# Grouped-query attention worked in pairs of heads, with its output GEMM given out between the pieces

## The chip, the core and the metric

The kernel runs on one core of one Trainium2 chip. The metric is the device time of one execution in microseconds (us); lower is better. The core's engines each work through a list of their own in program order and wait for each other at semaphores: PE (TensorE: matmuls and transposes), ACT (ScalarE), DVE (VectorE), POOL (GpSimd) and SP (SyncE, which here issues the weights' DMAs). PE has two clock levels, 1.2 and 2.4 GHz; the profile gives the granted clock as a share of the higher one, so 0.50 is the lower level and 1.00 the higher.

## The reference

The reference is two blocks one after the other on 256 tokens of width 1024: a hybrid block (differential attention, gated convolution, memory attention, an MLP), then two layers modulated by adaLN vectors. The change touches one step of the second block's first layer, grouped-query attention with 16 query heads of 64 features and 4 key/value heads, each of which serves 4 query heads:

```
def gqa_attention(h, w_qkv, q_g, k_g, w_o, cos, sin):
    B, T, _ = h.shape
    qkv = h @ w_qkv
    q, k, v = jnp.split(qkv, [Q_WIDTH, Q_WIDTH + KV_WIDTH], axis=-1)
    q = apply_rope(rmsnorm(q.reshape(B, T, N_HEADS, HEAD_DIM), q_g), cos, sin)
    k = apply_rope(rmsnorm(k.reshape(B, T, N_KV_HEADS, HEAD_DIM), k_g), cos, sin)
...
        s = jnp.einsum('bqkgd,bskd->bkgqs', q_blk, k).astype(jnp.float32) * scale
        p = jax.nn.softmax(s, axis=-1).astype(v.dtype)
        return jnp.einsum('bkgqs,bskd->bqkgd', p, v)
...
    return o @ w_o
```

## The kernel before

**Weights and GEMMs.** Every weight is streamed from HBM in loads of 1 MB and split into `whi` (rounded to fp32r, a cast on ACT, L86) and `wlo` (the exact rest, a subtraction on DVE, L87). The class `Weights` keeps these splits a few ahead of their use (`W.pump`, `W.rest`), and `W.cap` holds the order of the splits back where a stage has no use for them. A large GEMM makes three matmuls for each pair of operands (`mm3`, L397 to L399: hi by hi, hi by lo, lo by hi), each on 128x128 weights and 512 columns. The class `Rows` is a GEMM that goes by rows of the weights: `run(k, ...)` adds the k-th of eight blocks of 128 rows to four accumulators of [128, 512] in the pool `ps_a`. For the first two blocks it makes both token tiles at once; from the third block on it makes the first token tile up to block 5, holds the rest back, and makes it at the end, so that the first token tile is finished early and its normalisation can start (`L295` are the transposes of that).

**Attention, before.** After the projection of q, k and v, the 16 heads go one by one through five pieces. `gq_a` makes the scores of a head (L1254; operands of 64 rows, half of the array, both token tiles into one bank of `ps_a`), the negated row maximum `nm` (L752, DVE), the `bias` (L755, DVE) and two exponentials with row sums (L757, ACT, into `p`). `gq_b` makes the reciprocal of the sums (`rec`, L762, DVE) and scales the two halves of `p` by it (L764, DVE). `gq_t` transposes `p` by four matmuls with the identity (L771, PE) and copies the result into `pT` (L773, ACT). `gq_o` multiplies by the values (L1274, PE; an output of 64 columns, half of the array) and `gq_os` splits the finished pair of heads into the GEMM's operands `omT` hi (L277, a cast on ACT) and lo (L278, a subtraction on DVE). These matmuls are of plain fp32, and each is two passes in the profile: `x4` of L1254 or L1274 is two matmuls.

The function `slots` sets the order. In slot j, the AV product of head j-5, the transposes of head j-3, the scores of head j, the scaling of head j-1 and the split of head j-5 are issued in this order, which is also the order on every engine:

```
    slots(16, [[(5, gq_o), (3, gq_t), (0, gq_a), (1, gq_b), (5, gq_os)]])
```

The first few slots run as fillers inside the projection's last chunk, the others in a loop behind it, and only when all are through does the output GEMM `Rows("o2", 8)` start, with 96 matmuls on `omT`. The second half of q's rotary embedding (`rope`, L1191 to L1193, on DVE, and its transposes L680 on PE) falls between the first slots. The stage behind the output GEMM is the MLP `m2`, whose first matmul is of line L447.

Of the kernel before, what the change touches and what calls it, by code (L numbers as in the profile page):

```python
# [17 lines left out]
NT = 2  # L18
# [5 lines left out]
class Weights:  # L24
    """The weights in the order of their use: 1 MB loads, each split in two halves into
    operands hi (rounded to float32r) and lo (the exact rest)."""
# [66 lines left out]
    def first(self, kind, key):  # L93
        """The index of the first half of a load."""
        return 2 * next(i for i, u in enumerate(self.plan) if u[:2] == (kind, key))
# [8 lines left out]
    def done(self, rest=True):  # L104
        """One more half is used up: go on with the loads and splits (lo only up to rest() if told so)."""
# [7 lines left out]
def kernel(  # L113
# [28 lines left out]
    # ------------------------------------------------------------------ the weights' order  # L142
# [53 lines left out]
    # ------------------------------------------------------------------ loads at the start  # L196
# [63 lines left out]
    # ------------------------------------------------------------------ helpers  # L260
    def rsqrt(ss, inv, y, E=None):
        """y = 1/sqrt(ss*inv + EPS) by Newton's steps from the usual first guess."""
# [26 lines left out]
    def transposed(t, xn, gcol, bcol, dst):  # L289
        """A function that makes dst[hi, lo][:, :, tokens t] = (xn * g + b)^T, xn in two halves."""  # L290
# [38 lines left out]
    def norm(t, src, ssp, gcol, bcol, dst, E=None):  # L329
        """dst[hi, lo][:, :, tokens t] = (src over its root mean square * g + b)^T with g, b per feature;  # L330
        ssp: the sums of squares of src's halves. In three parts: this one, and two to be called later."""
# [32 lines left out]
    def later(n, f):  # L364
        """f runs n ticks on."""
        due.append((clock[0] + n, f))
# [40 lines left out]
    def gemm_cols(key, n0, act, evac, fill=1, acc=None, i0=0):  # L407
        """512 columns: act^T (tokens on partitions out) @ w; evac(the token tiles' psums)."""
# [13 lines left out]
    def gap():  # L422
        """A product that may run while TensorE would wait for operands."""
# [3 lines left out]
    def gemm_cols_skew(key, n0s, act, evacs, second, fill=1):  # L427
        """The first two of some chunks of columns: the first token tile runs six halves of weights
        ahead, while second() makes the operands of the other."""
# [36 lines left out]
    def gemm_cols_start(key, n0, act, evac, second, fill=1):  # L466
        """The first columns: two halves of weights for a token tile in turn; second() makes the operands
        of the other."""
# [22 lines left out]
    def gemm_feat(key, f0, act, p=ps_a, fill=1):  # L491
        """256 features: w^T @ act (features on partitions out), in one bank [2, 256 tokens]."""
# [765 lines left out]
    def gq_b(h):  # L1258
        softmax_b(*gq[h])
# [212 lines left out]
```

## Time and profile before

| | |
|---|---|
| Time, median of 3 runs | 1336.67 us |
| The three runs | 1336.67, 1340.35 and 1336.23 us |
| Span of the profiled execution | 1335.7 us (the profile gives no other time of it) |
| PE busy | 1315.5 us, 98% of the span |
| DVE, ACT busy | 926.9 us (69%), 731.2 us (55%) |
| Mean granted clock of PE | 0.992 |

The share of busy time is an average over many stages. The grouped-query attention and its output GEMM take some 73 us of the span, and what the change is worth has to be read from these 73 us. Start times in a timeline are us from the span's start. A matmul's "took" time overlaps its neighbours; what it costs in a chain is the distance from its start to the next start. In a timeline row the bracket at the end says how long the engine stood idle ahead of the row and what released it.

### The profile page before, as it was taken

What the parts mean: (1) busy time and instruction counts of PE and PEld (TensorE: products, weight loads), DVE (VectorE), ACT (ScalarE), POOL (GpSimd) and SP (SyncE); (2) the same over time, 40 slices, a digit from 0 to 9 for tenths busy, and PEclk for the clock granted to TensorE, in tenths of its full rate; (3) what the DMA queues carried; (4) which work ended last, traced back from release to release, by engine and by line L of the source; (5) the groups of instructions that cost most, each with busy time, mean ns of one, the idle gap of its engine ahead of it and who ended that gap; (6) DMA issues with size and microseconds to landing.
All of it is one profiled execution on the core that took longest, in us unless ns stands there. A gap on an engine that the chain in (4) does not pass through costs nothing.

```text
span 1335.7 us, 20533 instructions
## 1 busy us (share of the span) xinstructions
PE 1315.5 (98%) x7883; PEld 1141.9 (85%) x7883; DVE 926.9 (69%) x1424; ACT 731.2 (55%) x1184; POOL 140.0 (10%) x375
## 2 busy tenths in 40 slices
PE   8899999999999999999899999999999999999998
PEld 6788789999998889987657889987789988799896
DVE  5555678755776778777776787676888877764453
ACT  6765665554444655445575755445646543674451
POOL 1522154500001000100400000000000000000000
PEclk8999999999999999999899999999999999999999
DMA  6572344456885788984313687894886765465650
GB/s 235 201 247 95 127 149 163 154 199 217 269 273 173 237 293 288 285 305 144 110 63 111 200 297 254 269 315 151 292 269 222 253 229 194 135 208 187 214 190 32
DMA packets 166959, 275.43 MB, mean 206 GB/s; under 512 B 8412, under 2 KB 95244, under 8 KB 166732
## 3 DMA queue, kind: packets, MB, share of 16 engines
q1 hardware_dynamic: 137260, 219.78, 48.7%
q10 hardware_dynamic: 27808, 50.41, 11.5%
q0 software_dynamic: 1792, 3.92, 1.1%
q8 instruction: 62, 1.02, 0.3%
q14 instruction: 37, 0.30, 0.1%
HBM read 273.04 MB, written 1.05 MB: 205 GB/s over the span
## 4 chain that ended last, share of the span: by engine, by line
PE 93%; DMA 2%; POOL 1%; DVE 1%; ACT 1%; issue 1%; SPq 0%; ACTq 0%; DVEq 0%; POOLq 0%
PE bank L397 15%; PE bank L399 15%; PE bank L398 15%; PE bank L497 12%; PE bank L499 12%; PE bank L498 12%; PE bank L447 2%; PE bank L1274 1%; PE bank L1254 1%; PE bank L1386 1%; PE bank L438 1%; PE bank L771 1%; PE bank L295 1%; PE bank L680 1%; PE bank L1034 1%
## 5 line engine op out<-in xcount | busy, mean ns | idle before, releaser
L86 ACT CAST whi<-raw 128x1024 fp32r<-128x1024 f32 x412 | 426.3, 1051 | 277.1 <-PE bank L399 79.7
L87 DVE TENSOR_TENSOR wlo<-raw,whi 128x1024 fp32r<-128x1024 f32 x412 | 496.3, 1220 | 90.7 <-ACT whi L86 89.6
L497 PE MATMUL bank<-hT,whi 128*128 128x256 f32 x1152 | 328.6, 285 | 0.0
L499 PE MATMUL bank<-hT,wlo 128*128 128x256 f32 x1152 | 324.8, 282 | 0.0
L498 PE MATMUL bank<-hT,whi 128*128 128x256 f32 x1152 | 324.5, 282 | 0.0
L497 PEld LDWEIGHTS bank<-hT,whi 128*128 128x128 f32 x1152 | 216.5, 188 | 1.9 <-issue 1.3
L498 PEld LDWEIGHTS bank<-hT,whi 128*128 128x128 f32 x1152 | 217.5, 189 | 0.6
L499 PEld LDWEIGHTS bank<-hT,wlo 128*128 128x128 f32 x1152 | 217.1, 188 | 0.0
L397 PE MATMUL bank<-whi,act 128*128 128x512 f32 x384 | 152.2, 396 | 0.0
L398 PE MATMUL bank<-wlo,act 128*128 128x512 f32 x384 | 151.7, 395 | 0.0
L399 PE MATMUL bank<-whi,act 128*128 128x512 f32 x384 | 151.6, 395 | 0.0
L397 PE MATMUL bank<-whi,hT 128*128 128x512 f32 x308 | 128.2, 416 | 0.8 <-ACT hT L321 0.8
L399 PE MATMUL bank<-whi,hT 128*128 128x512 f32 x308 | 122.7, 398 | 0.0
L398 PE MATMUL bank<-wlo,hT 128*128 128x512 f32 x308 | 122.5, 398 | 0.0
L1018 DVE SCALAR_TENSOR_TENSOR acc<-araw,cond,acc 128x512 f32<-128x512 f32 x128 | 95.6, 747 | 27.4 <-DMA araw<-in_ada_w_dram 27.0
L399 PEld LDWEIGHTS bank<-whi,act 128*128 128x128 f32 x384 | 72.0, 187 | 17.5
L397 PEld LDWEIGHTS bank<-whi,act 128*128 128x128 f32 x384 | 72.0, 187 | 17.0
L398 PEld LDWEIGHTS bank<-wlo,act 128*128 128x128 f32 x384 | 72.0, 188 | 16.9
L397 PEld LDWEIGHTS bank<-whi,hT 128*128 128x128 f32 x308 | 58.3, 189 | 18.8 <-ACT hT L321 4.2
L399 PEld LDWEIGHTS bank<-whi,hT 128*128 128x128 f32 x308 | 58.4, 190 | 15.1 <-DVE hT L310 1.0
L398 PEld LDWEIGHTS bank<-wlo,hT 128*128 128x128 f32 x308 | 58.5, 190 | 13.5 <-issue 0.7
L278 DVE TENSOR_TENSOR act<-s,act 128x512 fp32r<-128x512 f32 x36 | 24.9, 691 | 58.2 <-ACT act L277 58.2
(298 smaller groups left out, 1893.9 us busy)
## 6 DMA issues: line engine op xcount, KB each, us to landing
araw<-in_ada_w_dram ACTq DMA_DIRECT2D x192, 256.0 KB
raw<-in_w_in_dram SPq DMA_DIRECT2D x40, 1024.0 KB
raw<-in_mlp_w_in_dram SPq DMA_DIRECT2D x32, 1024.0 KB
raw<-in_mlp_w_out_dram SPq DMA_DIRECT2D x32, 1024.0 KB
raw<-in_gmlp_w_in_dram SPq DMA_DIRECT2D x24, 1024.0 KB
raw<-in_w_mlp_in_dram SPq DMA_DIRECT2D x16, 1024.0 KB
raw<-in_w_mlp_out_dram SPq DMA_DIRECT2D x16, 1024.0 KB
raw<-in_gmlp_w_out_dram SPq DMA_DIRECT2D x12, 1024.0 KB
```

The source lines that it names most:

```text
L86: self.nc.scalar.copy(hv, v)
L87: self.rests.append(lambda v=v, hv=hv, lv=lv: self.nc.vector.tensor_sub(lv, v, hv.bitcast(F32)))
L278: V.tensor_sub(lo, src, hi.bitcast(F32))
L295: T.transpose(pss[g][:, j * P:(j + 1) * P], xn[g][:, j * P:(j + 1) * P], ident)
L397: T.matmul(acc, xh, wh, start=start, stop=False)
L398: T.matmul(acc, xh, wl, start=False, stop=False)
L399: T.matmul(acc, xl, wh, start=False, stop=stop)
L447: T.matmul(acc[c][0], act[e][:, k, 0:P], w[0][:, j, :], start=(k + e == 0), stop=False)
L497: T.matmul(acc[:, j], wh[:, k, :], act[0][:, k, :], start=(k == 0), stop=False)
L498: T.matmul(acc[:, j], wh[:, k, :], act[1][:, k, :], start=False, stop=False)
L499: T.matmul(acc[:, j], wl[:, k, :], act[0][:, k, :], start=False, stop=(k == 7))
L1018: V.scalar_tensor_tensor(acc, ada_st.pop(j), cond[:, k:k + 1], acc, op0=ALU.mult, op1=ALU.add)
```

## The change

Two heads are worked as one pair, eight pairs in all. `gq_scores` makes the scores of two heads in turn, one in the upper and one in the lower 64 rows of the array, each head into a bank of its own in the pool `ps_x`, then both `nm` and one `bias` for the pair. `gq_exp` makes the pair's four exponentials, `gq_norm` one reciprocal and four scalings, `gq_turn` the eight transposes, with one copy to `pT` on ACT and the other on DVE (before: both on ACT). `gq_out` multiplies both heads by the values, one in the left and one in the right 64 columns of the array, and splits the pair. `gq_pieces` sets three pieces for each j: the scores of pair j; the transposes of pair j-1 with the exponentials of pair j; the AV product of pair j-2 with the scaling of pair j. The output GEMM's block k starts as soon as pair k is through, and a piece is given out between its parts. Since the four accumulators of that GEMM now stand in `ps_a` at the same time, scores, transposes and AV products share the four banks of `ps_x`. The rest of the full diff takes out comments and docstrings. Its core:

```
@@ -503,10 +503,10 @@
         return acc
 
     class Rows:
-        def __init__(self, key, nk, skew=6):
-            self.key, self.nk, self.skew = key, nk, skew
+        def __init__(self, key, nk, skew=6, between=None):
+            self.key, self.nk, self.skew, self.between = key, nk, skew, between
             self.acc = None
             self.held = []
...
@@ -528,6 +528,8 @@
                 if k < self.nk - self.skew:
                     for t in range(NT):
                         self.mm(k, w, act, j, t)
+                        if self.between and t == 0:
+                            self.between()
                     W.done()
                     tick(fill)
                 else:
...
@@ -1247,65 +1249,96 @@
 
     gq = {}
 
-    def gq_a(h):
-        ps = bank(ps_a).rearrange("p (t k) -> p t k", t=2)
-        pr = slice(64 * (h % 2), 64 * (h % 2) + 64)
+    def gq_scores(p):
+        pss = [bank().rearrange("p (t k) -> p t k", t=2) for _ in range(2)]
         for t in range(NT):
-            T.matmul(ps[:, t], qT2[pr, h // 2, t * P:(t + 1) * P], kT2[pr, h // 4, :], start=True, stop=True)
-        p = attnp.tile([P, 2, 256], F32, tag="p", name="p", bufs=4)
-        gq[h] = p, softmax_a(ps, rsq2[:, :, h], p)
-    def gq_b(h):
-        softmax_b(*gq[h])
-    def gq_t(h):
-        pT = attnp.tile([P, 2, 256], F32, tag="pT", name="pT", bufs=3)
-        transpose_p(gq[h][0], pT.rearrange("p a b -> p (a b)"))
-        gq[h] = pT
-    def gq_o(h):
-        if h % 2 == 0:
-            gq["o"] = bank()
-        ps = gq["o"]
-        pT = gq.pop(h)
-        o0 = 64 * (h % 2)
-        kv = h // 4
+            for c in range(2):
+                pr = slice(64 * c, 64 * c + 64)
+                T.matmul(pss[c][:, t], qT2[pr, p, t * P:(t + 1) * P], kT2[pr, p // 2, :], start=True, stop=True)
+        nm = small.tile([P, 2, 2], F32, tag="nmg", name="nm")
+        for c in range(2):
+            V.tensor_reduce(nm[:, c], pss[c], axis=AX.X, op=ALU.max, negate=True)
+        bias = small.tile([P, 2, 2], F32, tag="biasg", name="bias")
+        V.tensor_mul(bias, nm, rsq2[:, :, 2 * p:2 * p + 2].rearrange("p t c -> p c t"))
+        gq[p] = pss, bias
+    def gq_exp(p):
+        pss, bias = gq[p]
+        sums = small.tile([P, 2, 2], F32, tag="sumsg", name="sums", bufs=4)
+        pt = [attnp.tile([P, 2, 256], F32, tag="p", name="p", bufs=4) for _ in range(2)]
+        for c in range(2):
+            for t in range(NT):
+                S.activation(pt[c][:, t], pss[c][:, t], AF.Exp, bias=bias[:, c, t:t + 1],
+                             scale=rsq2[:, t, 2 * p + c:2 * p + c + 1], accum_out=sums[:, c, t:t + 1])
+        gq[p] = pt, sums
+    def gq_norm(p):
+        pt, sums = gq[p]
+        rec = small.tile([P, 2, 2], F32, tag="recg", name="rec")
+        V.reciprocal(rec, sums)
+        for c in range(2):
+            for t in range(NT):
+                V.tensor_scalar(pt[c][:, t], pt[c][:, t], rec[:, c, t:t + 1], None, op0=ALU.mult)
+    def gq_turn(p):
+        pT = [attnp.tile([P, 2, 256], F32, tag="pT", name="pT", bufs=4) for _ in range(2)]
+        for c in range(2):
+            transpose_p(gq[p][0][c], pT[c].rearrange("p a b -> p (a b)"), on_act=(c == 0))
+        gq[p] = pT
+    def gq_out(p):
+        pT = gq.pop(p)
+        ps = bank()
+        vs = slice(64 * (p // 2), 64 * (p // 2) + 64)
         for kb in range(2):
-            T.matmul(ps[o0:o0 + 64, 0:256], v2[:, kb, 64 * kv:64 * kv + 64], pT[:, kb], start=(kb == 0), stop=(kb == 1))
-        gq[h, "o"] = ps
-    def gq_os(h):
-        ps = gq.pop((h, "o"))
-        if h % 2:
-            split_to(oT2[0][:, h // 2, :], oT2[1][:, h // 2, :], ps[:, 0:256])
+            for c in range(2):
+                T.matmul(ps[64 * c:64 * c + 64, 0:256], v2[:, kb, vs], pT[c][:, kb], start=(kb == 0), stop=(kb == 1))
+        split_to(oT2[0][:, p, :], oT2[1][:, p, :], ps[:, 0:256])
+    def gq_pieces():
+        for j in range(10):
+            for stage in ((gq_scores, 0, None, 0), (gq_turn, 1, gq_exp, 0), (gq_out, 2, gq_norm, 0)):
+                fs = [(f, j - lag) for f, lag in (stage[:2], stage[2:]) if f and 0 <= j - lag < 8]
+                if fs:
+                    yield j - 2 if stage[0] is gq_out else -1, fs
 
     rate, clock[1] = clock[1], 0.0
     fillers.append(rope_tables)
     W.cap = W.first("D", ("o2", 0))
     gemm_cols_skew("qkv2", (1024, 0), hT, (evac_kv2, evac_q2(0)), end)
-    fillers.extend([lambda: None] * 3)
-    slots(16, [[(5, gq_o), (3, gq_t), (0, gq_a), (1, gq_b), (5, gq_os)]])
     W.rest()
-    W.cap += 0
     gemm_cols("qkv2", 512, hT, evac_q2(1))
-    clock[1] = 0
-    n = 0
-    while fillers:
-        n += 1
-        if n > 2:
-            W.cap += 1
-            W.pump()
-            W.rest(1)
+    pieces = deque(gq_pieces())
+    def piece():
+        if pieces:
+            for f, p in pieces.popleft()[1]:
+                f(p)
+        W.cap += 1
+        W.pump()
+        W.rest(1)
         tick()
-    W.cap = 1 << 30
+    rows = Rows("o2", 8, between=piece)
+    for k in range(8):
+        while any(0 <= p <= k for p, _ in pieces):
+            piece()
+        piece()
+        if k == 2:
+            W.cap = 1 << 30
+            while len(ada) > 96:
+                ada.popleft()()
+        end = rows.run(k, [(oT2, k)], residual((0, 0), mods(0, 1)))
     clock[1] = 0.95
-    end = Rows("o2", 8).run(0, [(oT2, k) for k in range(8)], residual((0, 0), mods(0, 1)))
     g_st.close()
     end = mlp("m2i", "m2o", residual((0, 1), mods(1, 0)), end)
     ada_flush(48)
     clock[1] = 0.8
 
-    # ------------------------------------------------------------------ gated MLP with mixing over tokens
     gm_st = ExitStack()
     gmp = pool(gm_st, "gmlp")
     vg = gmp.tile([P, 2, 3072], F32, name="vg")
```

The lines of the two kernels differ: the scores are L1254 before and L1258 after, `nm` L752 and L1261, `bias` L755 and L1263, the exponentials L757 and L1272, `rec` L762 and L1279, the scalings of `p` L764 and L1282, the transposes L771 and L773, the copies of `pT` L773 and L775 (ACT) with L777 (DVE), and the AV product L1274 and L1297. In these rows a matmul counts once, not by its passes.

On DVE, one slot in the middle of the attention before, followed by the start of the next:

```order
L752 TENSOR_REDUCE nm<-bank 128x2
L755 TENSOR_TENSOR bias<-nm,rsq_6769 128x2
L762 RECIPROCAL rec<-sums 128x2
L764 TENSOR_SCALAR p<-p,rec 128x256 x2
L278 TENSOR_TENSOR omT_780<-bank,omT_779 128x256
L87 TENSOR_TENSOR wlo<-raw,whi 128x1024
L752 TENSOR_REDUCE nm<-bank 128x2
```

And on DVE in the middle of the attention now, one pair and the start of the next:

```order
L1279 RECIPROCAL rec<-sums 128x4
L1282 TENSOR_SCALAR p<-p,rec 128x256 x4
L1261 TENSOR_REDUCE nm<-bank 128x2 x2
L1263 TENSOR_TENSOR bias<-nm,rsq_6769 128x4
L777 COPY pT<-bank 128x512
L87 TENSOR_TENSOR wlo<-raw,whi 128x1024
L278 TENSOR_TENSOR omT_780<-bank,omT_779 128x256
L1279 RECIPROCAL rec<-sums 128x4
```

Before, `nm` and `bias` of a head stood ahead of the reciprocal and the scalings of the head before it. Now `nm` and `bias` of a pair stand behind the reciprocal and the scalings of the pair before it, and the subtraction that makes `omT` lo stands ahead of that reciprocal.

On ACT, two slots in the same place before:

```order
L757 ACTIVATE p,sums<-bank,bias,rsq_6769 128x256 x2
L86 CAST whi<-raw 128x1024
L773 COPY pT<-bank 128x512
L757 ACTIVATE p,sums<-bank,bias,rsq_6769 128x256 x2
L277 CAST omT_779<-bank 128x256
L773 COPY pT<-bank 128x512
```

And on ACT now, a pair with a weight's cast and a pair with the two DMA issues of the adaLN weights (L1001):

```order
L1272 ACTIVATE p,sums<-bank,bias,rsq_6769 128x256 x4
L86 CAST whi<-raw 128x1024
L277 CAST omT_779<-bank 128x256
L1001 DMA araw<-in_ada_w_dram 128x512 x2
L775 COPY pT<-bank 128x512
L1272 ACTIVATE p,sums<-bank,bias,rsq_6769 128x256 x4
```

The cast of `omT` hi stands behind the four exponentials of a later pair, and behind the weight's cast where there is one.

The start of the attention, on DVE before (L1191 to L1193 are the rotary embedding of q's second half):

```order
L752 TENSOR_REDUCE nm<-bank 128x2
L755 TENSOR_TENSOR bias<-nm,rsq_6769 128x2
L1191 TENSOR_TENSOR hf<-q_7109,ropeg 128x256 x2
L1192 TENSOR_TENSOR q_7109<-q_7109,ropeg 128x512
L1193 TENSOR_TENSOR q_7109<-q_7109,hf 128x512
L752 TENSOR_REDUCE nm<-bank 128x2
L755 TENSOR_TENSOR bias<-nm,rsq_6769 128x2
L762 RECIPROCAL rec<-sums 128x2
```

And the start on DVE now (the embedding is L1193 to L1195 here):

```order
L1195 TENSOR_TENSOR q_7109<-q_7109,hf 128x512
L87 TENSOR_TENSOR wlo<-raw,whi 128x1024
L1279 RECIPROCAL rec<-sums 128x4
L1282 TENSOR_SCALAR p<-p,rec 128x256 x4
L87 TENSOR_TENSOR wlo<-raw,whi 128x1024
L1193 TENSOR_TENSOR hf<-q_7109,ropeg 128x256 x2
L1194 TENSOR_TENSOR q_7109<-q_7109,ropeg 128x512
L1195 TENSOR_TENSOR q_7109<-q_7109,hf 128x512
L1261 TENSOR_REDUCE nm<-bank 128x2 x2
L1263 TENSOR_TENSOR bias<-nm,rsq_6769 128x4
```

Ahead of these rows stand the first pair's two `nm`, its `bias` and the first half of the embedding, as before. Between the first and the second pair's `nm` there are now two subtractions of `wlo` and the first pair's scalings; before, the second head's `nm` followed the embedding at once.

On PE, the start of the attention before (L680 are the transposes of the second half of q):

```order
L1254 MATMUL bank<-kT_6767,qT_6766 128x256 x6
L771 MATMUL bank<-ident,p 128x128 x4
L1254 MATMUL bank<-kT_6767,qT_6766 128x256 x2
L680 MATMUL bank<-ident,q_7109 128x128 x4
L771 MATMUL bank<-ident,p 128x128 x4
L1254 MATMUL bank<-kT_6767,qT_6766 128x256 x2
L1274 MATMUL bank<-pT,v_6768 64x256 x2
```

And on PE now, from the transposes of the first pair to the first part of the output GEMM (L682 is the L680 of before):

```order
L773 MATMUL bank<-ident,p 128x128 x8
L682 MATMUL bank<-ident,q_7109 128x128 x4
L1258 MATMUL bank<-kT_6767,qT_6766 128x256 x4
L773 MATMUL bank<-ident,p 128x128 x8
L1297 MATMUL bank<-pT,v_6768 64x256 x4
L1258 MATMUL bank<-kT_6767,qT_6766 128x256 x4
L397 MATMUL bank<-whi,omT_779 128x512
L398 MATMUL bank<-wlo,omT_779 128x512
L399 MATMUL bank<-whi,omT_780 128x512
L397 MATMUL bank<-whi,omT_779 128x512
L398 MATMUL bank<-wlo,omT_779 128x512
L399 MATMUL bank<-whi,omT_780 128x512
```

From here on a pair's transposes, AV product and scores and six of the GEMM's matmuls follow each other in turn. Six of the GEMM's matmuls stand in each pair's turn, 48 of the 96 in all; the other 48 come behind the last pair.

## Rows read from the trace of the kernel before

**Rows 1.** The page: the chain that ended last by engine, one costly group

```profile
PE 93%; DMA 2%; POOL 1%; DVE 1%; ACT 1%; issue 1%; SPq 0%; ACTq 0%; DVEq 0%; POOLq 0%
...
L1018 DVE SCALAR_TENSOR_TENSOR acc<-araw,cond,acc 128x512 f32<-128x512 f32 x128 | 95.6, 747 | 27.4 <-DMA araw<-in_ada_w_dram 27.0
```

**Rows 2.** Three stretches, us from the start: busy time of each engine, PE's clock

```profile
core 0: us, PE busy (x) PEld busy (x) DVE busy (x) ACT busy (x) POOL busy (x), PEclk, DMA share, GB/s
664.00:674.00 10.00, 10.00 (x29) 6.11 (x28) 8.00 (x19) 8.35 (x19) 1.91 (x4) 0.55 0.03 4
674.00:706.00 32.00, 32.00 (x150) 18.68 (x150) 23.00 (x67) 23.89 (x66) 0.00 (x0) 1.00 0.19 65
706.00:731.00 25.00, 25.00 (x114) 20.17 (x115) 15.91 (x30) 11.34 (x21) 0.00 (x0) 1.00 0.41 135
```

**Rows 3.** Timeline of PE: attention's start, a steady slot, the output GEMM, the next stage

```profile
663.03 1.08 PE L771 MATMUL bank<-ident,p 128*128 128x128 f32 x4 [3.51 <-DVE p L764]
664.05 2.07 PE L1254 MATMUL bank<-kT,qT 64*128 64x256 f32 x4
...
676.22 1.13 PE L1254 MATMUL bank<-kT,qT 64*128 64x256 f32 x4
677.27 1.08 PE L1274 MATMUL bank<-pT,v 128*64 128x256 f32 x4
678.28 0.65 PE L771 MATMUL bank<-ident,p 128*128 128x128 f32 x4
678.87 1.13 PE L1254 MATMUL bank<-kT,qT 64*128 64x256 f32 x4
...
707.72 0.50 PE L397 MATMUL bank<-whi,omT 128*128 128x512 f32 x1
708.07 0.40 PE L398 MATMUL bank<-wlo,omT 128*128 128x512 f32 x1
...
730.55 5.78 PE L447 MATMUL bank<-whi,hT 128*128 128x512 f32 x24
```

**Rows 4.** Timeline of PE: a pair of heads in row halves, differential attention

```profile
186.98 0.93 PE L866 MATMUL bank<-kT,qT 64*128 64x128 f32 x8
187.84 0.38 PE L497 MATMUL bank<-hT,whi 128*128 128x256 f32 x1
```

**Rows 5.** Timeline of DVE: attention's start, one slot, an `omT` lo

```profile
658.50 0.68 DVE L752 TENSOR_REDUCE nm<-bank 128x2 f32<-128x512 f32 x1
...
659.40 0.77 DVE L1191 TENSOR_TENSOR hf<-q,ropeg 128x256 f32<-128x256 f32 x2
...
661.54 0.68 DVE L752 TENSOR_REDUCE nm<-bank 128x2 f32<-128x512 f32 x1
...
681.33 0.68 DVE L752 TENSOR_REDUCE nm<-bank 128x2 f32<-128x512 f32 x1
682.05 0.16 DVE L755 TENSOR_TENSOR bias<-nm,rsq 128x2 f32<-128x2 f32 x1
...
682.32 0.61 DVE L764 TENSOR_SCALAR p<-p,rec 128x256 f32<-128x256 f32 x2
682.85 1.22 DVE L87 TENSOR_TENSOR wlo<-raw,whi 128x1024 fp32r<-128x1024 f32 x1
683.99 0.68 DVE L752 TENSOR_REDUCE nm<-bank 128x2 f32<-128x512 f32 x1
...
686.53 0.42 DVE L278 TENSOR_TENSOR omT<-bank,omT 128x256 fp32r<-128x256 f32 x1 [0.86 <-ACT omT L277]
```

**Rows 6.** Timeline of ACT: one slot's exponentials and cast, an `omT` hi

```profile
682.31 0.56 ACT L757 ACTIVATE p<-bank,bias,rsq 128x256 f32<-128x256 f32 x1 [1.05 <-DVE rec L762]
...
682.86 0.55 ACT L757 ACTIVATE p<-bank,bias,rsq 128x256 f32<-128x256 f32 x1
...
683.41 1.04 ACT L86 CAST whi<-raw 128x1024 fp32r<-128x1024 f32 x1
...
686.13 0.36 ACT L277 CAST omT<-bank 128x256 fp32r<-128x256 f32 x1
```

## The prediction, made before the changed kernel was run

> **What bounds the kernel now.** I read the page first: PE ends 93% of the chain that ended last [rows 1]. That is a share over the whole span, so I went to the 73 us of grouped-query attention by windows and by PE's timeline. The reader is to see three stretches there. Until 663.03 PE has scores to make but then stands idle for 3.51 us, because the transposes wait for the first scaled `p` of DVE [rows 3]. From 664 to 674 PE is busy all the time, but at a granted clock of 0.55, which is the 1.2 GHz level for most of it; four passes of the scores took 2.07 us there against 1.13 us later [rows 2, 3]. From 674 to 731 PE is busy all the time at clock 1.00, while DVE is busy 23.00 of 32 us and ACT 23.89 of 32 [rows 2]. So the steady part is bound by PE. A slot costs 2.65 us of PE (676.22 to 678.87): 1.05 us for the scores, 1.01 for the AV product, 0.59 for the transposes [rows 3]. The other two engines use three quarters of it, a head at a time, with a slack that a pipeline over five heads can use.
>
> The output GEMM takes 707.72 to 730.55, that is 22.83 us for 96 matmuls and one set of eight transposes [rows 3], or about 0.23 us a matmul (22 us for the 96, the rest for the transposes). The next stage begins at 730.55, again with matmuls, and since PE ends 93% of the whole chain [rows 1], I take it that a shift of this point is kept to the end. **What the change is worth is how far this 730.55 moves.**
>
> **What it removes from PE.** Two heads in the two halves of the array run side by side. The trace has this already in differential attention: eight passes of L866, four of 128 and four of 256 columns, start at 186.98 and the next matmul at 187.84, so they took 0.86 us [rows 4]. Four passes of 256 columns alone cost 1.05 us here and four of 128 columns (the transposes) 0.59 us [rows 3], 1.64 us one after the other. So a pair costs a little over half, and I take the scores of a pair at 1.05 us where two heads cost 2.10, and in the same way the AV products at 1.01 us instead of 2.02. Over eight pairs that is 8 x (1.05 + 1.01) = 16.5 us less work on PE. Column halves of this shape do not stand in these rows; the bounds are 1.01 us (as with row halves) and 2.02 us (no gain). I take the first and keep the second as a rival. The GEMM's matmuls and the transposes cost the same as before: a pair's share on PE is 1.05 + 1.01 + 2 x 0.59 + 6 x 0.23 = 4.6 us.
>
> **What it adds, on DVE and ACT.** No operation is added there; eight of 16 `bias` and eight of 16 reciprocals fall away. What moves is their order, and here I part from PE's sum. Before, `nm` and `bias` of a head are ahead of the scalings of the head before it, so ACT always had the next exponentials to do while DVE scaled. Now, on DVE, a pair's `nm` and `bias` stand behind the reciprocal and the scalings of the pair before, which wait for that pair's last exponential; and the subtraction for `omT` lo stands ahead of the reciprocal and waits for the cast of `omT` hi, which on ACT stands behind these same four exponentials. So ACT and DVE take turns and nothing of one pair lies beside the next. One turn, by starts:
>
> - reciprocal to first scaling: `bias`, reciprocal and hand-over together take 682.05 to 682.32; 0.2 us for one of the two;
> - four scalings: two take 682.32 to 682.85, so 2 x 0.53 = 1.06 us;
> - two `nm`: about 0.6 us for the first and 0.72 for the second up to `bias` (681.33 to 682.05), 1.32 us [rows 5];
> - `bias` to the first exponential: 682.05 to 682.31, 0.26 us [rows 5, 6];
> - four exponentials: 682.31, 682.86, 683.41, so 4 x 0.55 = 2.20 us;
> - `omT` hi, from its start to that of the subtraction: 686.13 to 686.53, 0.40 us [rows 5, 6];
> - the subtraction: 0.42 us long, 0.34 up to the next instruction [rows 5].
>
> The sum is 5.78 us, more than PE's 4.6. So PE will wait about a microsecond in each pair, and the loop of the two other engines sets the pace.
>
> Some pairs cost more. A weight's cast in ACT's row ahead of `omT` hi adds about 1.0 us (1.04 us long) [rows 6]; by the order that is so in two pairs, the fourth and the fifth. Behind the fifth, ACT issues two loads of adaLN weights; the second refills a buffer that DVE must first read, in an instruction of 0.75 us like L1018's [rows 1], and this stands behind `nm` and `bias`. The copy of `pT` and the exponentials stand behind these issues on ACT, so the sixth pair costs about 1.3 us more. On SP and POOL nothing changes places.
>
> **The sum.** Everything up to the first score matmul is as before, and so is the first `nm` at 658.50 [rows 5].
>
> - First reciprocal: 658.50 + 1.32 (two `nm`) + 0.1 (`bias`) + 2.14 (half an embedding, 659.40 to 661.54) + 1.14 (`wlo`, 682.85 to 683.99) = 663.2 [rows 5].
> - Second reciprocal: 0.2 + 1.06 + 1.14 (`wlo`) + 2.14 (embedding) + 1.32 + 0.26 + 2.20, and 0.4 to hand the sums over = 8.7, so 671.9.
> - Third: 0.2 + 1.06 + 1.14 (`wlo`) + 1.32 + 0.26 + 2.20 + 0.40 + 0.34 = 6.9, so 678.8. The first part of the output GEMM begins here, and not before.
> - Fourth and fifth, with a cast: 2 x 6.8, so 692.4. Sixth: 7.1, so 699.5. Seventh and eighth: 2 x 5.8, so the last reciprocal is at 711.1.
> - Then the last scalings (1.26) and the last four transposes (0.6) to 713.0; six matmuls of the GEMM (1.4) cover the copy of `pT`; 714.4; the last two pairs' AV products, 2 x 1.0; 716.4.
> - Then `omT` hi and lo of these two pairs, about 0.4 + 2 x 0.34, and a `wlo` behind them on DVE, 1.14: 718.6. Four matmuls of the other half of the GEMM fit ahead of that `wlo`; the other 44 and the eight transposes take 22.83/2 + about 0.4 - 4 x 0.23 = 10.9 us.
>
> The next stage then begins at 729.5, 1 us earlier than 730.55. **16.5 us come off PE's work, and 15 of them become waits**: in the start (before, PE bridged 664 to 674 with work at half clock; now it waits), and a microsecond or two in each of eight pairs.
>
> One term is left: **the clock**. The 10 us of half level before stand behind the idle time of 3.51 us [rows 2, 3]. Now PE has such idle times from 659 to 679 again and again, with little work between, so I expect the low level for most of that stretch, where it costs nothing, since the other engines set the pace. It costs where it lasts into the steady pairs: a pair at half level is 2 x 4.6 = 9.2 us on PE, against a loop of 6.8, so 2.4 us for each such pair. Since PE is then busy without a pause, as from 664 to 674, it should recover as it did there. None to two such pairs: 0 to 4.8 us; I take 1.6, near the lower third. The stage then begins at 731.1, 0.5 us later than before. The span, 1335.7 us, would be 1336.2; the median of the runs stands 1.0 us above this profiled span, and I carry that over: **1337.2 us**.
>
> **A rule against the change.** The trace says it by the loop's rows. The Trainium skill, "TensorEngine Tiling (Array Packing)", section "PSUM Bottleneck", says that packing speeds up TensorE but not the evacuation of PSUM, which may become the bottleneck. By matmul rows alone the sum is the first rival's; by the rule it is the one above, since every score is still read from PSUM twice (`nm`, exponentials) at the old rate; by that rule, rows and forecast agree.
>
> **The rivals.** About 0.3%, 4.0 us, is what a measurement of this kernel can tell from no change.
>
> - *PE stays the bound* (faster). The 16.5 us come off in full: 1336.7 - 16.5 = 1320. For it: DVE and ACT are idle a quarter of the steady part [rows 2]. Against it: the turn above is a chain, and idle time of its engines is of no use to it. It decides from a turn of 5.2 us down: 8 x 0.6 less is 4.8 us, so 1332.4. I give it, with everything between, 0.16.
> - *The clock stays low* (slower). PE waits in every pair, and if that holds the lower level to the last pair, PE becomes the bound again at 9.2 us a pair: against the steady pairs' 39 us from 672 to 711, five or six pairs at 9.2 cost 50 us, 12 us more, so 1349. Against it: at that level PE has no pause, and before it recovered within 10 us of that. From two such pairs on, 4.8 us, it is slower in the sense above: 1340.4 and up. Chance 0.18.
> - *The halves do not run side by side* (the change does not do what it says). A pair then is 4.6 + 2.06 = 6.7 us on PE, about the same as the turn with a cast; the three or four plain turns of 5.8 become 6.7, some 3 us more: 1340. Against it stand the 0.86 us of [rows 4]. Chance 0.06, inside the band of no change.
>
> **How the numbers follow.** The loop as summed has 0.60, and lies in 1333 to 1341; with the halves' case the band of no change has 0.66. Faster 0.16, slower 0.18. For 8 in 10 the range reaches a little into both: 1332 to 1343 us.
>
> **What the new profile would show.** Right: the first matmul of the output GEMM near 679; PE idle a microsecond or two per pair ahead of the transposes, released by DVE's `p`; reciprocals 5.8 us apart, 6.8 with a cast, and the exponentials waiting for DVE's `bias`; the score passes of a pair in about 1.1 us; L447 within 3 us of 730.5. Wrong: reciprocals under 5.2 us apart or PE without pauses after 680 (then faster); a granted clock near 0.5 behind 690 (then slower); score passes of 2.1 us at clock 1.00 (the halves). If the next stage's start has moved but the time has not, or the other way round, the reason lies outside what I summed.

## The result

| | before | changed |
|---|---|---|
| Time, median | 1337.82 us (4 runs) | 1321.82 us (1321.23 to 1325.46, 4 runs) |
| Ratio to before | | 0.9885, 95% interval 0.9872 to 0.9898 |
| Span of the profiled execution | 1335.7 us | 1319.5 us |

The changed kernel is 16 us faster, and the time lies outside the range of 1332 to 1343 us. Its page begins with these lines on the busy times (busy us, share of the span, instructions) and on the chain that ended last:

```profile
span 1319.5 us, 20492 instructions
...
PE 1282.4 (97%) x7883; PEld 1118.4 (85%) x7883; DVE 929.4 (70%) x1416; ACT 725.9 (55%) x1176; POOL 141.8 (11%) x375
...
PE 73%; DMA 9%; DVE 8%; ACT 4%; POOL 2%; issue 2%; ACTq 0%; SPq 0%; DVEq 0%; POOLq 0%
```

PE is busy 33 us less, twice what pairing takes off its work, and PE's share of the last chain has fallen from 93% [rows 1] to 73%. So the first place to look is where in the span the 16 us lie. I took the same instruction in both traces at several points and compared its start. These are, of the kernel before, rows of DVE's timeline, one 14 us ahead of the first score matmul and one at the end:

```profile
642.80 0.42 DVE L1219 TENSOR_TENSOR kn<-kd,rskv 128x256 f32<-128x256 f32 x1 [2.91 <-POOL rskv L274]
...
1329.91 0.69 DVE L1095 TENSOR_TENSOR hf<-bank,gate 128x512 f32<-128x512 f32 x1 [5.58 <-PE bank L399]
```

And these of the changed kernel, in the same timeline:

```profile
636.85 0.43 DVE L1221 TENSOR_TENSOR kn<-kd,rskv 128x256 f32<-128x256 f32 x1 [3.48 <-POOL rskv L274]
...
1313.77 0.69 DVE L1097 TENSOR_TENSOR hf<-bank,gate 128x512 f32<-128x512 f32 x1 [5.58 <-PE bank L399]
```

Between them, in its timeline of PE, the first matmul behind the attention:

```profile
724.59 5.66 PE L447 MATMUL bank<-whi,hT 128*128 128x512 f32 x24
```

**The changed kernel is already 5.95 us ahead before the changed code begins.** Behind the attention it is 5.96 us ahead (730.55 [rows 3] to 724.59), and at the end 16.14. The attention and its GEMM, between the first and the second point, gained nothing. All of the 16 us were won in code that did not change, a little everywhere. PE's timeline near 300 us shows what a little is: the first and the last of six matmuls of the 256-column form, in the kernel before and then in the changed one:

```profile
299.80 0.28 PE L497 MATMUL bank<-hT,whi 128*128 128x256 f32 x1
...
300.40 0.28 PE L499 MATMUL bank<-hT,wlo 128*128 128x256 f32 x1
```

```profile
299.74 0.28 PE L498 MATMUL bank<-hT,whi 128*128 128x256 f32 x1
...
300.31 0.28 PE L497 MATMUL bank<-hT,whi 128*128 128x256 f32 x1
```

Five steps from start to start take 0.60 us before and 0.57 us now, 0.120 and 0.114 each, at the same granted clock of 1.00. Over the whole trace the mean step between neighbours on hT of this form is 0.1210 us before and 0.1164 now, pauses included (0.1200 and 0.1153 without them); with 512 columns it is 0.2342 and 0.2295, pauses left out. There are 3456 matmuls of the first form (three lines of 1152): 3456 x 4.6 ns = 15.9 us. Some 1060 steps of the second give 5.0 us more, and part of the sum is lost again in waits for other engines: PE now waits 1.8 us for `wlo` in the line of `act` (L398), where its page showed 0.0 before.

**In the attention itself** the turn of ACT and DVE is there as predicted. Rows of DVE's timeline in the changed kernel, its eight reciprocals and between two of them one whole turn:

```profile
657.22 0.17 DVE L1279 RECIPROCAL rec<-sums 128x4 f32<-128x4 f32 x1
657.42 1.75 DVE L1282 TENSOR_SCALAR p<-p,rec 128x256 f32<-128x256 f32 x4
...
666.62 0.17 DVE L1279 RECIPROCAL rec<-sums 128x4 f32<-128x4 f32 x1
...
673.47 0.17 DVE L1279 RECIPROCAL rec<-sums 128x4 f32<-128x4 f32 x1
...
680.12 0.17 DVE L1279 RECIPROCAL rec<-sums 128x4 f32<-128x4 f32 x1
680.33 1.14 DVE L1282 TENSOR_SCALAR p<-p,rec 128x256 f32<-128x256 f32 x4
681.39 1.28 DVE L1261 TENSOR_REDUCE nm<-bank 128x2 f32<-128x512 f32 x2
682.77 0.17 DVE L1263 TENSOR_TENSOR bias<-nm,rsq 128x4 f32<-128x4 f32 x1
...
686.51 0.42 DVE L278 TENSOR_TENSOR omT<-bank,omT 128x256 fp32r<-128x256 f32 x1 [1.84 <-ACT omT L277]
686.85 0.17 DVE L1279 RECIPROCAL rec<-sums 128x4 f32<-128x4 f32 x1
...
694.13 0.17 DVE L1279 RECIPROCAL rec<-sums 128x4 f32<-128x4 f32 x1
...
700.62 0.17 DVE L1279 RECIPROCAL rec<-sums 128x4 f32<-128x4 f32 x1
...
706.33 0.17 DVE L1279 RECIPROCAL rec<-sums 128x4 f32<-128x4 f32 x1
```

The turn with a weight's cast takes 6.73 us (680.12 to 686.85; 6.8 forecast), the plain one 5.71 (700.62 to 706.33; 5.8 forecast), and in the first of these DVE waits 1.84 us for ACT's cast of `omT`. The rows of PE beside it, its timeline and three windows (the columns as in [rows 2]):

```profile
676.98 1.08 PE L1297 MATMUL bank<-pT,v 128*64 128x256 f32 x8
678.00 1.14 PE L1258 MATMUL bank<-kT,qT 64*128 64x256 f32 x8
679.80 0.50 PE L397 MATMUL bank<-whi,omT 128*128 128x512 f32 x1 [0.67 <-ACT omT L277]
...
691.35 1.59 PE L1297 MATMUL bank<-pT,v 128*64 128x256 f32 x8 [2.29 <-ACT pT L775]
692.87 2.08 PE L1258 MATMUL bank<-kT,qT 64*128 64x256 f32 x8
...
707.03 1.25 PE L773 MATMUL bank<-ident,p 128*128 128x128 f32 x8 [2.83 <-DVE p L1282]
```

```profile
657.00:673.00 16.00, 11.12 (x44) 7.06 (x44) 13.89 (x27) 10.92 (x26) 3.31 (x9) 0.57 0.40 131
673.00:705.00 32.00, 26.56 (x154) 17.71 (x154) 21.83 (x54) 16.56 (x50) 0.00 (x0) 0.95 0.16 50
705.00:725.00 20.00, 17.04 (x88) 13.21 (x89) 14.42 (x33) 10.09 (x23) 0.00 (x0) 1.00 0.27 87
```

Eight passes of a pair's scores take 1.14 us at full clock, where four took 1.13 [rows 3]: the halves do run side by side. PE is idle 5.4 of the 32 us from 673 to 705, and waits for `omT` and `pT`, and a little later for `p`.

### The profile page after: what moved, and what is told of

The parts are those of the page before. It is cut to its first block, busy times and chain, and to the rows that moved or that the text cites. A ratio compares the mean times of both kernels' runs of the same rounds, so it can differ in the third digit from the quotient of the medians.

```text
span 1319.5 us, 20492 instructions
## 1 busy us (share of the span) xinstructions
PE 1282.4 (97%) x7883; PEld 1118.4 (85%) x7883; DVE 929.4 (70%) x1416; ACT 725.9 (55%) x1176; POOL 141.8 (11%) x375
## 4 chain that ended last, share of the span: by engine, by line
PE 73%; DMA 9%; DVE 8%; ACT 4%; POOL 2%; issue 2%; ACTq 0%; SPq 0%; DVEq 0%; POOLq 0%
PE bank L397 12%; PE bank L399 12%; PE bank L398 12%; PE bank L497 9%; PE bank L498 9%; PE bank L499 9%; DMA araw<-in_ada_w_dram 6%; DVE wlo L87 3%; PE bank L447 2%; ACT whi L86 1%; PE bank L1419 1%; DMA raw<-in_w_mem_kv_dram 1%; ACT p L1272 1%; PE bank L438 1%; DVE gate L1020 1%
## 5 line engine op out<-in xcount | busy, mean ns | idle before, releaser
L497 PE MATMUL bank<-hT,whi 128*128 128x256 f32 x1152 | 324.1, 281 | 0.0
L498 PE MATMUL bank<-hT,whi 128*128 128x256 f32 x1152 | 320.6, 278 | 0.0
L499 PE MATMUL bank<-hT,wlo 128*128 128x256 f32 x1152 | 320.5, 278 | 0.0
L398 PE MATMUL bank<-wlo,act 128*128 128x512 f32 x384 | 152.1, 396 | 1.8 <-DVE wlo L87 1.8
L399 PE MATMUL bank<-whi,act 128*128 128x512 f32 x384 | 151.8, 395 | 0.0
L399 PE MATMUL bank<-whi,hT 128*128 128x512 f32 x308 | 121.6, 395 | 0.0
L398 PE MATMUL bank<-wlo,hT 128*128 128x512 f32 x308 | 121.1, 393 | 0.0
L398 PEld LDWEIGHTS bank<-wlo,act 128*128 128x128 f32 x384 | 72.2, 188 | 19.8 <-DVE wlo L87 3.1
L399 PEld LDWEIGHTS bank<-whi,act 128*128 128x128 f32 x384 | 72.1, 188 | 17.3
L399 PEld LDWEIGHTS bank<-whi,hT 128*128 128x128 f32 x308 | 58.3, 189 | 14.0 <-DVE hT L310 1.0
L398 PEld LDWEIGHTS bank<-wlo,hT 128*128 128x128 f32 x308 | 58.4, 189 | 12.5 <-issue 1.0
```

The source lines that it names most:

```text
L398: T.matmul(acc, xh, wl, start=False, stop=False)
L399: T.matmul(acc, xl, wh, start=False, stop=stop)
L497: T.matmul(acc[:, j], wh[:, k, :], act[0][:, k, :], start=(k == 0), stop=False)
L498: T.matmul(acc[:, j], wh[:, k, :], act[1][:, k, :], start=False, stop=False)
L499: T.matmul(acc[:, j], wl[:, k, :], act[0][:, k, :], start=False, stop=(k == 7))
```

## The experiments

What can make matmuls faster that nobody touched? The changed kernel takes four new kinds of small tiles (`nmg`, `biasg`, `sumsg`, `recg`: 3 + 3 + 4 + 3 = 13 tiles of 32 bytes per partition) from the pool `small`, and the buffers that are allocated behind this pool move up by 13 x 32 = 416 bytes. The built kernels have the first `whi` at byte 72192 of a partition before, and at 72608 now; `raw`, `wlo`, `omT` and the scratch tiles moved with it, `hT` at 26464 and the activations at the other end (`act`, `mgT`, `cvT`, `oT`) did not. My theory became that where the buffers lie makes the gain; the rival, that the new order of the attention does.

**pad416**, the kernel before with 416 unused bytes:

```diff
     gq = {}
+    V.memset(small.tile([P, 104], F32, tag="pad", name="pad", bufs=1), 0.0)
```

> The kernel before, its attention unchanged, with one unused tile of 416 bytes per partition (and one memset of it) in the pool of small vectors, so that the raw weights, their split operands and most later buffers lie 416 bytes higher, where the changed kernel has them. Theory of the addresses: the gain lies in where the buffers lie, not in the attention; about 1322 us, and the matmuls of line L497 start 0.116 us apart instead of 0.120. Rival, the attention's new order acts on the whole program in some way: 1337 us and 0.120.

Measured: 1321.41 us, ratio 0.9874 (0.9857 to 0.9890). Without any change of the attention the whole gain is there, and the mean step on hT is 0.1164 us, as in the changed kernel.

**after_unshifted**, the changed kernel with its small tiles elsewhere (the same for `biasg`, `sumsg` and `recg`):

```diff
-        nm = small.tile([P, 2, 2], F32, tag="nmg", name="nm")
+        nm = attnp.tile([P, 2, 2], F32, bufs=3, tag="nmg", name="nm")
```

> The changed kernel with its 13 new small tiles taken from the attention's own pool, so that the weights' buffers lie where the kernel before has them. Theory of the addresses: the gain is gone, 1336 to 1338 us, since the attention itself then brings the 0 to 1 us that its rows show. Rival: 1322 us as the changed kernel.

Measured: 1338.48 us, ratio 1.0003 (0.9994 to 1.0012). The change of the attention by itself is worth nothing that can be measured here, although PE's page total is 1302.0 us, 13.5 less than before: what pairing took off PE became waits. The two runs together settle where the gain is from.

**pad32** and **pad256**, as pad416 with `[P, 8]` and `[P, 64]`, one run each:

> The kernel before with an unused tile of 32 bytes. If what counts is that the weights' buffers no longer begin at a multiple of 64 bytes, about 1322 us as with 416. If it is a larger distance between buffers, 1337 us. If addresses do not count, 1337 us.

> The kernel before with an unused tile of 256 bytes: the buffers begin at a multiple of 64 and of 256 bytes still, but not of 512. If the 64 bytes count, 1337 us; if 512 bytes or the distance to the operands that did not move count, a time between 1322 and 1337 us.

Measured: 1334.33 us and 1339.37 us. 256 bytes do nothing and 32 a part: neither of my readings for 32 fits fully, but a rule that repeats after 256 bytes or a divisor of it fits both. The time of the one run with 32 bytes also understates its matmuls. Counted by PE's own order, its 3668th matmul starts 4.67 us earlier than before, near 568 us, and the 3930th 2.74 us later, near 628. In between PE waited 3.9 us for `wlo` and was then at the lower clock level for 6.8 us, which the kernel before does not have there (windows of pad32, then of the kernel before, with the columns of [rows 2]):

```profile
602.00:610.00 8.00, 6.46 (x17) 4.98 (x17) 5.08 (x11) 2.00 (x6) 0.00 (x0) 0.57 0.64 208
```

```profile
602.00:610.00 8.00, 8.00 (x36) 6.42 (x35) 6.33 (x16) 3.67 (x7) 0.00 (x0) 1.00 0.65 223
```

**pad160**, **shift_split** and **shift_behind**: 160 bytes in the same place; 416 bytes between the raw weights and their split operands; 416 bytes behind the split operands (the edit of shift_split; in shift_behind the line of `gapp` stands one line further down):

```diff
     w_raw = pool(ctx, "wraw", Weights.RAW)
+    gapp = pool(ctx, "gapp")
     w_split = pool(ctx, "wsplit", Weights.SPLIT)
...
+    V.memset(gapp.tile([P, 104], F32, name="pad"), 0.0)
```

> The kernel before with an unused tile of 160 bytes per partition in the pool of small vectors; 160 is 416 less 256, and 256 changed nothing. Theory that the place within 256 bytes counts: 1321 us, as with 416. Theory that only the place within 64 bytes counts (160, 416 and 32 are alike in it): as with 32, about 1334 us or, where that run was held back by something else, 1322 us.

> The kernel before with 416 unused bytes between the raw weights and their split operands, so that the raw weights stay where they were and whi, wlo and all behind them move. If the place of PE's operands whi and wlo counts: 1322 us. If that of the raw weights counts, into which the loads write: 1337 us.

> The kernel before with 416 unused bytes behind the split operands: raw, whi and wlo stay, and only the buffers behind them (omT, the scratch tiles, the adaLN loads) move. If whi and wlo count: 1337 us. If the buffers behind count: 1322 us, or part of the way where omT alone counts.

Measured: pad160 1322.72 us, ratio 0.9879 (0.9856 to 0.9902); shift_split 1323.33 us, 0.9884 (0.9864 to 0.9903); shift_behind 1339.62 us, 1.0011 (0.9994 to 1.0029). So the place of `whi` and `wlo` counts, within 256 bytes; that of the raw weights and of the buffers behind does not show.

**probe**, a kernel of nothing but matmuls in the two forms, with weights in one tile W and activations in one tile X, both from a multiple of 256 bytes on; one line of the kernel for each pair of offsets, here the weights at 0 and the activations at 192 bytes (48 floats):

```diff
+    [T.matmul(bk[2][:, 0:256], W[:, 0 + 128 * (k // 3):0 + 128 * (k // 3) + 128], X[:, 48 + 256 * (k // 3):48 + 256 * (k // 3) + 256], start=(k == 0), stop=(k == 23)) for k in range(24)]
```

> PE's matmuls by themselves; the reference is not computed (the output is a constant). Two shapes: 128 columns of weights with 256 moving columns, 24 in a row as in lines L497 to L499, and 512 moving columns as in L397 to L399. The base of the weights' tile (s) and of the activations' tile (m) is moved in steps of 32 bytes through 256. First PE alone, for all 64 pairs of s and m; then with ACT and DVE making splits of 128x1024 beside it, into tiles at 0 and then at 160 bytes past a multiple of 256. If PE's reads of its own two operands disturb each other, the spacing of starts varies with s and m while PE is alone, between about 0.115 and 0.122 us. If it is the writes and reads of ACT and DVE that disturb PE, the spacing is the same for all s and m while PE is alone, and varies with s once the splits run. If it is the loads' writes, no stretch here shows it.

Its timeline of PE, with PE alone. L62 to L69 have the weights at 0 and the activations at 0, 32, ... 224 bytes; L102 and L105 have the weights at 160 and the activations at 0 and 96. A line's cost is the distance to the next line's start:

```profile
15.91 3.04 PE L62 MATMUL bank<-X,W 128*128 128x256 f32 x24
18.78 3.00 PE L63 MATMUL bank<-X,W 128*128 128x256 f32 x24
21.61 2.99 PE L64 MATMUL bank<-X,W 128*128 128x256 f32 x24
24.44 3.03 PE L65 MATMUL bank<-X,W 128*128 128x256 f32 x24
27.31 3.01 PE L66 MATMUL bank<-X,W 128*128 128x256 f32 x24
30.16 2.98 PE L67 MATMUL bank<-X,W 128*128 128x256 f32 x24
32.98 2.89 PE L68 MATMUL bank<-X,W 128*128 128x256 f32 x24
35.70 3.00 PE L69 MATMUL bank<-X,W 128*128 128x256 f32 x24
38.54 3.00 PE L70 MATMUL bank<-X,W 128*128 128x256 f32 x24
...
129.33 3.04 PE L102 MATMUL bank<-X,W 128*128 128x256 f32 x24
132.21 3.02 PE L103 MATMUL bank<-X,W 128*128 128x256 f32 x24
...
137.88 2.89 PE L105 MATMUL bank<-X,W 128*128 128x256 f32 x24
140.61 3.00 PE L106 MATMUL bank<-X,W 128*128 128x256 f32 x24
```

L62 takes 2.87 us, L65 (96 bytes apart) 2.87, L68 (192 apart) 2.72. With the weights at 160, the slow place is at 0 (2.88 us; 0 less 160 is 96 modulo 256) and the fast one at 96 (2.73; 96 less 160 is 192). The mean step inside such a line, over all 64 pairs, is nearly a function of one number, the place of the moving operand less that of the stationary one, modulo 256; at 160 and at 192 the eight places of the weights give more than one step:

| moving less stationary, bytes | 0 | 32 | 64 | 96 | 128 | 160 | 192 | 224 |
|---|---|---|---|---|---|---|---|---|
| step with 256 columns, weights at 0, us | 0.1197 | 0.1180 | 0.1180 | 0.1196 | 0.1187 | 0.1174 | 0.1137 | 0.1180 |
| lowest of the eight places of the weights | 0.1197 | 0.1177 | 0.1178 | 0.1196 | 0.1184 | 0.1173 | 0.1137 | 0.1180 |
| highest of the eight | 0.1197 | 0.1180 | 0.1180 | 0.1200 | 0.1190 | 0.1186 | 0.1178 | 0.1184 |

Beside the splits of ACT and DVE the pair at weights 0, activations 96 takes 0.1198 and the pair at 32 and 96 takes 0.1178, as without. So the slow step needs no splits. But the changed kernel's own pair, weights at 160 and activations at 96, takes 0.1178 beside them, both times that it was run, and 0.1137 alone; its line L160 takes 2.83 us, where L105 took 2.73:

```profile
278.47 2.99 PE L160 MATMUL bank<-X,W 128*128 128x256 f32 x24
281.30 2.98 PE L161 MATMUL bank<-X,W 128*128 128x256 f32 x24
```

The changed kernel has both steps. Near 300 us five of them took 0.57 us, and here five take 0.59 us, at the same granted clock of 1.00:

```profile
1002.90 0.28 PE L497 MATMUL bank<-hT,whi 128*128 128x256 f32 x1
...
1003.49 0.28 PE L499 MATMUL bank<-hT,wlo 128*128 128x256 f32 x1
```

Each unbroken run of these matmuls on hT keeps to one of the two: 1937 steps of 0.113 to 0.114 us and 1414 of 0.118, where the kernel before has 0.120 in all its runs. It is not the splits that choose between them there, since the mean is 0.1154 with a cast of ACT and a subtraction of DVE alongside and 0.1151 with neither. What chooses is open, and so is whether the weights' own place does at 192, where the probe ran each pair once with PE alone.

The kernel before has hT at 96 and the weights at 0 past a multiple of 256, distance 96, one of the two slowest; the changed kernel has the weights at 160, distance 192, which has the lowest step of all (0.1137) and 0.1178 as its other. pad32 has distance 64, and a step between the two: 0.1183 in its trace, beside 0.1210 and 0.1164 of the two kernels, pauses included in all three. With 512 columns, where hT is the stationary operand, the same measurement gives 0.2344 us for the places of before (weights 0, hT 96), 0.2299 for those of now (160, 96), and 0.2267 to 0.2286 where both lie at the same place.

**ht_moved** tells the distance from the weights' own place: hT moves, the weights stay at a multiple of 256:

```diff
+    V.memset(const.tile([P, 24], F32, name="padh"), 0.0)
     hT = [const.tile([P, 8, 256], F32R, name=f"hT{i}") for i in range(2)]
...
+    V.memset(small.tile([P, 40], F32, tag="pad", name="pad", bufs=1), 0.0)
```

> The kernel before with the operand hT moved instead of the weights: 96 unused bytes ahead of hT and 160 behind it, so that hT lies at 192 past a multiple of 256 and the weights at 0 as before. Theory of the distance (what counts is where the moving operand lies relative to the weights, within 256 bytes; hT less whi is 192 here as in the changed kernel): 1322 us and L497 at 0.114 to 0.116 us. Rival, the weights' own place counts: 1337 us and 0.120.

Measured: 1322.89 us, ratio 0.9872 (0.9856 to 0.9888), and 0.1166 us a step on hT. The distance counts.

**cast_dve** goes back to the attention and tests the turn, on the changed kernel:

```diff
-        split_to(oT2[0][:, p, :], oT2[1][:, p, :], ps[:, 0:256])
+        V.tensor_copy(oT2[0][:, p, :], ps[:, 0:256])
+        V.tensor_sub(oT2[1][:, p, :], ps[:, 0:256], oT2[0][:, p, :].bitcast(F32))
```

> The changed kernel with the omT hi cast of each pair made by DVE, ahead of the subtraction, and not by ACT behind the four exponentials of a later pair. Theory of the turn (ACT and DVE take turns in each pair): the hand-over of 0.4 us and, in two pairs, the weight's cast of 1 us leave the turn, about 0.5 us a pair and 1.4 in those two; the next stage's first matmul comes 4 to 6 us earlier, and the time is 1316 to 1318 us. Rival, PE or the four banks set the pace there: 1321 to 1322 us.

Measured: 1317.99 us, ratio to before 0.9845 (0.9828 to 0.9861), 3.8 us less than the changed kernel, or 5 by the two ratios; the profiled execution is the lowest of its four (1314.28). DVE's timeline, one plain turn, and PE's, the next stage:

```profile
693.25 0.42 DVE L1298 CAST omT<-bank 128x256 fp32r<-128x256 f32 x1 [0.59 <-PE bank L1297]
...
694.42 0.18 DVE L1279 RECIPROCAL rec<-sums 128x4 f32<-128x4 f32 x1 [0.29 <-ACT p L1272]
...
699.54 0.18 DVE L1279 RECIPROCAL rec<-sums 128x4 f32<-128x4 f32 x1 [0.28 <-ACT p L1272]
```

```profile
717.87 0.39 PE L447 MATMUL bank<-whi,hT 128*128 128x512 f32 x1
```

The turn is 5.12 us instead of 5.71, and its reciprocal waits for the exponentials alone. The next stage starts 6.7 us earlier than in the changed kernel (724.59), of which 2.0 were there ahead of the attention (first reciprocal at 655.25 instead of 657.22); so the attention gave 4.7 us, within the 4 to 6 expected.

**before_layout** and **best** use the distance for the other operands. 64 unused bytes at the other end bring `act`, `mgT`, `cvT` and `oT` from 224 to 160, where the weights are; before_layout is pad160 with it, best is cast_dve with it:

```diff
+    V.memset(pool(ctx, "rpad", side="right").tile([P, 16], F32, name="rpad"), 0.0)
     memp = pool(right, "memp", side="right")
```

> The kernel before, its attention unchanged, with the weights at 160 past a multiple of 256 and with 64 unused bytes at the other end of the buffer space, which bring the activations of L397 to L399 (act and three more) from 224 to 160 too, so that weights and activations have distance 0 there. By the measurement of PE alone these matmuls then start 0.228 us apart instead of 0.233: some 1400 of them, about 7 us beyond the 1322 us of the shift by 160, so 1314 to 1316 us. Rival, PE's spacing is hidden there by other work: 1321 to 1323 us.

> The changed kernel with the omT cast on DVE and the 64 unused bytes at the other end: the two gains together, 1318 less 7, so 1310 to 1313 us. Rival, as there: 1317 to 1319 us.

Measured: before_layout 1318.60 us, ratio 0.9844 (0.9823 to 0.9865); best 1312.92 us, 0.9799 (0.9781 to 0.9817). The step on `act` fell from 0.2333 to 0.2270 us in both, over 1152 matmuls 7.3 us, as the probe has it. Of that some 4 us reach the time from pad160 to before_layout, less than I expected (1314 to 1316); the intervals of the two ratios overlap a little. From cast_dve to best it is 5 us, with intervals apart. Two losses show in the rows of before_layout: 2.5 us that PE waits for `wlo` in the line of `act` (L399), and `cvT` and `oT`, which the 64 bytes bring to distance 0 in the form with 256 columns, where their step rises from 0.1178 to 0.1197 us, 0.7 us over 384 matmuls. best is the fastest of all, 26 us under the kernel before that ran beside it (1338.80).

## Why the prediction was wrong

Point by point, by its steps:

- **The turn.** Forecast gaps between the reciprocals 8.7, 6.9, 6.8, 6.8, 7.1, 5.8, 5.8; measured 9.40, 6.85, 6.65, 6.73, 7.28, 6.49, 5.71. Right in the turn, and cast_dve changed it as the mechanism says. The first gap is 0.7 longer: DVE's four scalings at 657.42 took 1.75 us where the sum had 1.06, and no run shows why. The sixth is 0.7 longer too: ACT's exponentials stand behind its copy of `pT` at 697.20, which waits for PE's transposes, and PE had made its scores in 2.08 us at 692.87, at the lower clock level. The first two pairs' turns hold 12 of the GEMM's matmuls each and the next four 6, so PE's share is about 6.0 us in the two turns with a cast, still less than the 6.65 and 6.73 measured.
- **The pairs side by side.** Right: 1.14 us for a pair's scores; 1.08 for its AV product at full clock (676.98), as long as for one head before [rows 3].
- **The tail.** From the last reciprocal to L447, 18.4 us forecast, 18.26 measured (706.33 to 724.59).
- **The clock.** From 657 to 673 it is 0.57, the 1.2 GHz level for most of it, behind an idle time of PE of 3.19 us at 656.31; from 673 to 705 it is 0.95, with the low level again only from 691.8 to 695.2. It stood low mostly where DVE set the pace (busy 13.23 of 13.6 us from 657.7), as I expected, and bears on the time only in the sixth gap. I took 1.6 us for it, and with it the sum for the attention came out at +0.5 us. The two points around the attention give 0.0 here; in after_unshifted, 0.13 us ahead at the first (642.67) and 0.31 behind at L447 (730.86), they give +0.4.
- **The sum.** My 1337.2 us, 0.5 above the median before, took every duration outside the attention as it was before. In after_unshifted they are, and it has 1338.48 us at a ratio of 1.0003, which is 0.4 above.

The step that failed stands ahead of the sum: "Everything up to the first score matmul is as before", and behind it that a shift of 730.55 is kept to the end, with every duration outside the 73 us taken over from the trace of before. The order of the instructions is indeed the same there, but their durations are not: the 3456 matmuls on hT of the 256-column form step by 0.1164 us and not by 0.1210, 15.9 us in all, so DVE is 5.95 us ahead before the attention starts and the shift of 730.55, 5.96 us, grows to 16.14 at the end. The prediction's last sign of being wrong, that this start and the time do not move together, did show it. The diff takes 13 more tiles from a pool that is allocated ahead of the weights' buffers, and I read these lines for what they compute and not for what they move. No rival had this mechanism. That the first rival's 1320 us is close to the measured time is luck: PE is not the bound of the attention, which has the waits and the turn of the forecast.

That the changed distance makes the gain is shown by pad416, after_unshifted, shift_split and shift_behind, and ht_moved; that the step depends on it with no other engine at work, by the probe. What happens inside PE or the memory to make it so, and why distance 192 has two steps, stays open.

## What to carry to other kernels

Before forecasting from a diff, ask what it moves in memory as well as in time: a few small tiles in an early pool shift every buffer behind them, and in this kernel, whose PE is busy 98% of the span, 4 ns a matmul were worth more than a stage's reordering. Compare first the start of one and the same instruction ahead of the changed code; if it has moved already, look at what else the change touched before you credit the new order. And in a pipeline over several engines, look whether an engine's instructions for the next piece stand behind those that wait for this one: that turn, and not the engines' idle shares, set the pace here.

## What the runs showed of the hardware

- The step between matmuls depends on where the two operands lie relative to each other modulo 256 bytes: 0.1137 to 0.1200 us with 256 fp32r columns and PE alone (5.5%). Beside the splits of ACT and DVE at full clock the probe has 0.1173 to 0.1202. With 512 columns it is 0.2267 to 0.2286 us at distance 0 and 0.2344 at the worst that the probe met. Moving both operands together changed the step with 256 columns by at most 0.0006 us, but for the distances 160 (0.1173 to 0.1186) and 192 (0.1137 to 0.1178).
- At distance 192 one and the same pair of places has two steps: 0.1137 us alone and 0.1178 beside the splits in the probe (weights at 160, activations at 96), and both, 1937 and 1414 times, in the changed kernel.
- The distance with the lowest step is not the same for both forms: 192 bytes for 256 columns, 0 for 512 (with the activations at 0, 96 and 224 bytes).
- Two heads in two row halves, eight passes of 256 columns, take 1.14 us, as long as four passes of one head (1.13 [rows 3]).
